# Keys of the latent attention projected with features in rows, tables on ACT and DVE, low parts on Pool

## The chip, the cores and the metric

The kernel runs on one core of one Trainium2 chip. The metric is the device time of one launch in microseconds; the time of the kernel before is the median of 3 runs. The engines are TensorE (PE), VectorE (DVE), ScalarE (ACT), GpSimd (Pool) and the queue that issues transfers (SP).

## What is computed

A decoder of two layers on 256 tokens of width 1024, all in float32. Each layer has three causal attentions side by side and a gated feed-forward part:

```python
h = rms_norm(x, attn_norm)
aq, ak, av, bq, bk, bv, c_q, c_kv_pe, gates = split(h @ w_in)
y_a = diff_attention(aq, ak, av, lam, ...) @ w_branch_a      # 4 heads, two softmaxes each
y_b = dilated_attention(bq, bk, bv, ...) @ w_branch_b        # 4 heads of 128
y_c = mla(c_q, c_kv_pe, ...) @ w_branch_c                    # 8 heads of 64 + 32 rotated
x = x + (g_a * y_a + g_b * y_b + g_c * y_c) @ w_out
x = x + (silu(h2 @ w_ffn_gate) * (h2 @ w_ffn_up)) @ w_ffn_down
```

In `mla` the latent c_q (384) is normalised and expanded to the queries of 8 heads. The latent c_kv (256) is normalised and expanded to 8 heads of 64 key and 64 value features, `kv = (rms_norm(c_kv) @ w_ukv).reshape(B, S, 8, 128)`. A further key part of 32 features is rotated by position and shared by all heads.

## The kernel before

**Products.** Every float32 operand is split in a high part of reduced width and a low part, the rest; a product is three matmuls, high by high, high by low and low by high (`mm3`, `mm` at L210). The high part is made by ACT (`hi_of`, L223) and the low part by DVE, as the source less the high part (`lo_of`, L228, with a scale L230). The weights, 156 MB in all, stream from HBM into five tiles `raw`; ACT makes `whi` from each and DVE `wlo`, five of each.

**Dense stream.** `dense(l)` is a generator. It holds the products of the layer's first half in a fixed order: the latent part of w_in, the projection of queries and keys for a (`qk_proj`, 4 steps), the expansion of the latents (`mla_up`: queries in 3 pieces, keys and values in 2), the values for a (`v_proj`), queries and keys for b, values for b, then the branch products. `pump(n)` runs it for n pieces. Its results stand in four PSUM banks, `bank`; another four, `att`, serve the attention.

**Attention.** `attention()` has 16 units (4 of a, 8 of c, 4 of b), each in stages: scores, softmax terms, transposes of the probabilities, values. The stages run with fixed lags against one another, and after each step one piece of the dense stream is pumped. It begins after 16 pieces of the stream from `latent_scaled` on in layer 0 (1 + 1 + 1 + 13) and 17 in layer 1. A score unit costs DVE two custom instructions (L757), ACT two exponentials (L759).

**Order.** The instructions are not issued in the order of the code: a scheduler of the Tile framework simulates the engines' queues and sets the order on every engine. The order within one queue is then fixed.

**The latent part.** `latent_factors` makes the factors rq and rk of the norms (Pool, L372) and rotates the shared key part on Pool (`rope`, L602 to L605) into `kpe`, from which it is copied to all heads of `k_tm` (L684). `mla_up` projects queries into four banks and scales them by rq into `q_tm`, tokens in rows (L563); Pool rotates their last 32 features in place. Then it projects keys and values together, tokens in rows, in four banks `pu[b][f]`: 24 matmuls of 512 columns in a layer. Each bank is read by ACT for the keys (L588, into `k_tm`, times rk) and by ACT and DVE for the values (into `vc`), and put back at once. `head_pair` (L719) transposes two heads of `q_tm` and two of `k_tm`, 4 transposes each, and splits the results. Pool also makes the distance tables `ta` and `tb` of the scores (L338, L342, L343). `low` are the low parts of the stacked keys for a, DVE's.

## Time and profile before

| | |
|---|---|
| time, median of 3 runs | 883.58 us (883.51 to 883.76) |
| the profiled execution's own time | 883.18 us |
| its span, first to last instruction | 881.4 us |
| PE busy | 873.6 us, 99% |
| DVE busy | 591.1 us, 67% |
| ACT busy | 502.2 us, 57% |
| Pool busy | 71.4 us, 8% |
| mean granted clock of TensorE | 0.999 |

The profile shows one execution. Start times are counted from the span's start. Matmuls overlap in the pipeline, so the time that one takes of PE is the distance between two starts, not its duration. On DVE and ACT too the next instruction starts somewhat before the last one ends.

### The profile page before, as it was taken

The page shows a single profiled execution, that of the slowest core. Times are in us where ns is not written, and L with a number is a line of the kernel's source. Part 1 is how long each engine was busy: PE and PEld are TensorE (multiplying, and loading weights), DVE is VectorE, ACT ScalarE, POOL GpSimd, SP SyncE. Part 2 cuts the span into 40 slices and gives each one's busy share as a digit, 9 for nine tenths or more (in the row PEclk, how much of TensorE's full clock was granted, in tenths as well). Part 3 has the DMA queues.
Part 4 walks back from the last instruction along what each step waited for, and adds up shares of the span by engine and source line. Part 5 has one row for each costly group of instructions (what it writes and reads, how often), then busy time and mean ns, then how long its engine had stood idle before and what let it go on. Part 6 is the DMA issues. An engine that isn't in the chain of part 4 may idle for free.

```text
span 881.4 us, 12736 instructions
## 1 busy us (share of the span) xinstructions
PE 873.6 (99%) x4710; PEld 759.5 (86%) x4710; DVE 591.1 (67%) x990; ACT 502.2 (57%) x852; POOL 71.4 (8%) x95
## 2 busy tenths in 40 slices
PE   9999999999999999999999999999999999999997
PEld 9989988888888888888899899888888888888886
DVE  5988878665666655555467888786556666656444
ACT  7797777644454444444376867775454644444332
POOL 1940310000000000000011303100000000000000
PEclk9999999999999999999999999999999999999999
DMA  9756444456656665656475553444555556655541
GB/s 340 245 170 209 128 141 160 146 169 193 187 167 197 187 190 182 182 186 191 127 226 174 172 168 128 151 145 159 180 189 182 167 193 202 203 190 180 181 141 49
DMA packets 45423, 155.92 MB, mean 177 GB/s; under 512 B 5168, under 2 KB 6192, under 8 KB 45360
## 3 DMA queue, kind: packets, MB, share of 16 engines
q1 hardware_dynamic: 44928, 154.55, 55.0%
q8 instruction: 37, 0.61, 0.3%
q10 hardware_dynamic: 432, 0.55, 0.2%
q14 instruction: 26, 0.21, 0.1%
HBM read 154.03 MB, written 1.05 MB: 176 GB/s over the span
## 4 chain that ended last, share of the span: by engine, by line
PE 97%; POOL 1%; issue 1%; DVE 0%; ACT 0%; POOLq 0%
PE bank L210 87%; PE att L210 6%; PE att L445 2%; PE att L719 1%; PE att L767 0%; PE att L768 0%; PE att L769 0%; POOL f L602 0%; PE att L693 0%; PE att L851 0%; POOL f L604 0%; POOL f L603 0%; POOL q_tm L605 0%; DVE x_tm L1043 0%; ACT x_tm L1058 0%
## 5 line engine op out<-in xcount | busy, mean ns | idle before, releaser
L210 PE MATMUL bank<-whi,fr 128*128 128x512 f32 (+1 forms) x2032 | 631.1, 387 | 0.0
L228 DVE TENSOR_TENSOR wlo<-raw,whi 128x1024 fp32r<-128x1024 f32 (+2 forms) x294 | 353.9, 1206 | 250.8 <-ACT whi L223 250.1
L223 ACT ACTIVATE whi<-raw 128x1024 fp32r<-128x1024 f32 (+2 forms) x294 | 305.0, 1041 | 305.8 <-PE bank L210 246.0
L210 PEld LDWEIGHTS bank<-whi,fr 128*128 128x128 f32 x2032 | 379.8, 188 | 71.5 <-ACT whi L223 0.2
L210 PE MATMUL bank<-wlo,fr 128*128 128x512 f32 (+1 forms) x1016 | 390.1, 386 | 0.0
L210 PEld LDWEIGHTS bank<-wlo,fr 128*128 128x128 f32 x1016 | 191.0, 188 | 35.5 <-DVE wlo L228 0.3
L210 PE MATMUL bank<-fr,whi 128*128 128x256 f32 x512 | 94.6, 285 | 0.0
L210 PEld LDWEIGHTS bank<-fr,whi 128*128 128x128 f32 x512 | 80.0, 192 | 0.2
L210 PE MATMUL bank<-fr,wlo 128*128 128x256 f32 x256 | 73.0, 285 | 0.0
L210 PEld LDWEIGHTS bank<-fr,wlo 128*128 128x128 f32 x256 | 49.0, 192 | 0.0
L372 POOL TENSOR_TENSOR r<-small,mhalf 128x2 f32<-128x2 f32 x4 | 2.8, 708 | 477.5 <-DVE small L398 462.6
L759 ACT ACTIVATE s<-s,small 128x256 f32<-128x256 f32 (+1 forms) x80 | 35.8, 455 | 1.2 <-DVE small L757 0.8
L372 POOL TENSOR_TENSOR small<-small,mhalf 128x2 f32<-128x2 f32 (+1 forms) x12 | 10.0, 831 | 280.5 <-DVE small L1047 178.5
L223 ACT ACTIVATE fr<-att 128x512 fp32r<-128x512 f32 (+2 forms) x54 | 28.3, 559 | 4.1 <-PE att L719 2.3
L210 PE MATMUL att<-whi,fr 128*128 128x288 f32 (+1 forms) x108 | 29.9, 290 | 0.0
L228 DVE TENSOR_TENSOR fr<-att,fr 128x512 fp32r<-128x512 f32 (+2 forms) x46 | 28.2, 634 | 0.1
L223 ACT ACTIVATE fr<-f 64x512 fp32r<-64x512 f32 (+2 forms) x40 | 23.3, 583 | 6.7 <-DVE f L516 5.4
L210 PE MATMUL att<-fr,fr 96*128 96x256 f32 (+3 forms) x152 | 26.0, 277 | 0.0
L210 PEld LDWEIGHTS att<-fr,fr 96*128 96x128 f32 (+1 forms) x152 | 22.7, 190 | 0.6
L615 ACT ACTIVATE f<-bank,rh 128x512 f32<-128x512 f32 x24 | 16.3, 689 | 11.7 <-PE bank L210 11.7
L972 ACT ACTIVATE f<-bank,rh 128x512 f32<-128x512 f32 (+1 forms) x24 | 15.6, 654 | 12.2 <-PE bank L210 12.2
L210 PEld LDWEIGHTS att<-whi,fr 128*128 128x128 f32 x108 | 20.4, 191 | 0.1
(134 smaller groups left out, 636.0 us busy)
## 6 DMA issues: line engine op xcount, KB each, us to landing
raw<-w SPq DMA_DIRECT2D x272, 512.0 KB, 3.6
raw<-w SPq DMA_DIRECT2D x16, 336.0 KB, 3.2
raw<-w SPq DMA_DIRECT2D x6, 384.0 KB, 3.6
x_tm<-xt SPq DMA_DIRECT2D x2, 512.0 KB, 6.4
f<-x SPq DMA_DIRECT2D x3, 256.0 KB, 5.2
f<-fnorm SPq DMA_DIRECT2D x2, 256.0 KB, 4.2
out<-x_tm ACTq DMA_DIRECT2D x2, 256.0 KB, 2.2
f<-x SPq DMA_DIRECT2D x2, 128.0 KB, 3.1
```

Of the source, the lines that this page charges most:

```text
L210: self.nc.tensor.matmul(out, lhsT, rhs, start=start, stop=stop, skip_group_check=True)
L223: self.nc.scalar.activation(out=hi, in_=src, func=AF.Copy, scale=scale)
L228: self.nc.vector.tensor_tensor(out=lo, in0=src, in1=h, op=ALU.subtract)
L372: self.nc.gpsimd.tensor_tensor(out=out, in0=v, in1=self.mhalf[:, 0:v.shape[1]], op=ALU.pow)
L445: self.nc.tensor.transpose(ps[:, c, b * 128:b * 128 + 128], src[b][:, c0 + c * 128:c0 + c * 128 + 128], self.ident)
L615: nc.scalar.activation(out=t[b], in_=bank[b], func=AF.Tanh, scale=self.rh[:, b:b + 1])
L719: nc.tensor.transpose(ps[0:96, c, b * 128:b * 128 + 128], src[:, b, 2 * p + c, :], self.ident)
L759: nc.scalar.activation(out=s[:, SL[b]], in_=s[:, SL[b]], func=AF.Exp, bias=mn[:, b:b + 1], scale=-1.0, accum_out=z[:, b:b + 1])
L972: nc.scalar.activation(out=a, in_=g, func=AF.Tanh, scale=self.rh[:, b:b + 1])
```

## The change

The columns of the kv weights are sorted on the host: keys of all heads first, then values. Keys are projected with features in rows: in each layer 24 matmuls of 256 columns into two banks `pk`, and 12 of 512 for the values into two banks `pv`. The factor rk is applied to the latent beforehand (`latent_factors`, now ahead of the transposes of the latents). Each head's keys are split out of the bank into `kc` (ACT and DVE, 64x256, head by head), the values of a token block in one step of each engine. All four banks are put back after the last split. The rotated key part is transposed (2 transposes a layer) and split into rows 64 to 95 of `kc` (`keys_placed`). `head_pair` transposes queries only. Tables: `ta` on ACT, `tb` on DVE. The low parts of the keys in `low`, and of queries and keys for b, go to Pool (`lo_pool`). The attention begins after 19 pieces in layer 0 (1 + 1 + 1 + 1 + 15) and 20 in layer 1. The last line of the diff gives room in SBUF.

```diff
+    def lo_pool(self, lo, src, hi):
+        self.nc.gpsimd.tensor_tensor(out=lo, in0=src, in1=hi.bitcast(F32), op=ALU.subtract)
...
-        self.k_tm = cp.tile([128, 2, 8, 96], F32, name="k_tm")
+        self.kc = cp.tile([128, 8, 2, 256], F32R, name="kc")
...
-        self.kpe = cp.tile([128, 2, 32], F32, name="kpe")
+        self.kpe = cp.tile([128, 2, 96], F32, name="kpe")
+        nc.gpsimd.memset(self.kpe, 0.0)
...
         for h in range(4):
             t = cp.tile([128, 256], F32, name=f"ta{h}")
-            nc.gpsimd.tensor_scalar(out=t, in0=dm[:, 0:256], scalar1=SLOPE_A[h], scalar2=None, op0=ALU.mult)
+            nc.scalar.activation(out=t, in_=dm[:, 0:256], func=AF.Copy, scale=SLOPE_A[h])
...
         for h in range(4):
             t = cp.tile([128, 256], F32, name=f"tb{h}")
-            nc.gpsimd.tensor_scalar(out=t, in0=db[:, 0:256], scalar1=SLOPE_B[h], scalar2=None, op0=ALU.mult)
-            nc.gpsimd.tensor_tensor(out=t, in0=t, in1=db[:, 256:512], op=ALU.subtract)
+            nc.vector.scalar_tensor_tensor(out=t, in0=db[:, 0:256], scalar=SLOPE_B[h], in1=db[:, 256:512], op0=ALU.mult,
+                                           op1=ALU.subtract)
...
-    def key_pair(self, src, rows=slice(0, 128)):
+    def key_pair(self, src, rows=slice(0, 128), pool=False):
         kd = self.fr.pair()
-        self.split(*fields(kd[rows]), src)
+        hi, lo = fields(kd[rows])
+        self.hi_of(hi, src)
+        (self.lo_pool if pool else self.lo_of)(lo, src, hi)
         return kd
...
         for c in range(2):
             self.hi_of(out[c][halves[1 - c]], t[halves[c]])
-            self.lo_of(self.low[j - 2][c][halves[c]], t[halves[c]], out[c][halves[c]])
+            self.lo_pool(self.low[j - 2][c][halves[c]], t[halves[c]], out[c][halves[c]])
...
             elif j < 2:
                 hi, lo = self.fr.get(), self.fr.get()
-                self.split(hi, lo, t)
+                self.hi_of(hi, t)
+                self.lo_pool(lo, t, hi)
                 q.append((hi, lo))
             else:
-                k.append(self.key_pair(tv))
+                k.append(self.key_pair(tv, pool=True))
             self.f.put(t)
...
         yield
-        pu = [[self.banks.get() for _ in range(2)] for _ in range(2)]
+        banks = [self.banks.get() for _ in range(4)]
+        pk, pv = banks[0:2], banks[2:4]
+        hi, lo = self.ck
         for k in range(2):
             (wh, wl), = self.take()
+            ts = slice(k * 256, k * 256 + 256)
+            for p in range(4):
+                s = slice(p * 128, p * 128 + 128)
+                self.mm3(pk[p // 2][:, (p % 2) * 256:(p % 2) * 256 + 256], wh[:, s], wl[:, s], hi[:, ts], lo[:, ts],
+                         k == 0 and p % 2 == 0, k == 1)
             for b in range(2):
-                h, lo = (t[:, k * 256 + b * 128:k * 256 + b * 128 + 128] for t in self.ck)
-                for lhs, ww, s, e in ((h, wh, k == 0, False), (h, wl, False, False), (lo, wh, False, k == 1)):
-                    for f in range(2):
-                        self.mm(pu[b][f], lhs, ww[:, f * 512:f * 512 + 512], s, e)
+                h, l = (t[:, k * 256 + b * 128:k * 256 + b * 128 + 128] for t in self.ck)
+                self.mm(pv[b], h, wh[:, 512:1024], k == 0, False)
+                self.mm(pv[b], h, wl[:, 512:1024], False, False)
+                self.mm(pv[b], l, wh[:, 512:1024], False, k == 1)
             if k < 1:
                 yield
         self.fr.put(*self.ck)
+        for p in range(4):
+            for c in range(2):
+                src = pk[p // 2][c * 64:c * 64 + 64, (p % 2) * 256:(p % 2) * 256 + 256]
+                self.split(self.kc[0:64, 2 * p + c, 0], self.kc[0:64, 2 * p + c, 1], src)
         for b in range(2):
-            for f in range(2):
-                kv = pu[b][f].rearrange("p (h d) -> p h d", h=4)
-                s = self.rk[:, b:b + 1]
-                nc.scalar.activation(out=self.k_tm[:, b, 4 * f:4 * f + 4, 0:64], in_=kv[:, :, 0:64], func=AF.Copy, scale=s)
-                hi, lo = (self.vc[b][:, 4 * f:4 * f + 4, i] for i in range(2))
-                self.split(hi, lo, kv[:, :, 64:128], s)
-                self.banks.put(pu[b][f])
+            self.split(self.vc[b][:, :, 0], self.vc[b][:, :, 1], pv[b].rearrange("p (h d) -> p h d", h=8))
+        self.banks.put(*banks)
         yield
...
     def latent_factors(self, l):
...
+        for v in (self.vq, self.vk):
+            nc.vector.tensor_scalar(out=v, in0=v, scalar1=EPS, scalar2=None, op0=ALU.add)
         self.rq = self.cp.tile([128, 2], F32, name=f"rq{l}")
-        self.rk = self.cp.tile([128, 2], F32, name=f"rk{l}")
-        rq = self.small()
+        rk, rq = self.small(), self.small()
+        self.rsqrt(rk, self.vk)
         self.rsqrt(rq, self.vq)
-        self.rsqrt(self.rk, self.vk)
+        for b in range(2):
+            nc.vector.tensor_scalar(out=self.cks[b][:, 0:256], in0=self.cks[b][:, 0:256], scalar1=rk[:, b:b + 1],
+                                    scalar2=None, op0=ALU.mult)
         nc.vector.tensor_scalar(out=self.rq, in0=rq, scalar1=-(96 ** -0.5), scalar2=None, op0=ALU.mult)
...
+    def turned_keys(self):
+        nc = self.nc
         for b in range(2):
             t1, t2 = self.f.get(), self.f.get()
-            kp = self.kpe[:, b]
+            kp = self.kpe[:, b, 64:96]
             nc.gpsimd.tensor_copy(kp, self.cks[b][:, 256:288])
             self.rope(kp, t1[:, 0:32], t2[:, 0:32], b, [128])
             self.f.put(t1, t2)
-            nc.gpsimd.tensor_copy(self.k_tm[:, b, :, 64:96], kp.unsqueeze(1).to_broadcast([128, 8, 32]))
+        self.f.put(*self.cks)
+
+    def keys_placed(self):
+        ps = self.att.get()
+        for b in range(2):
+            self.nc.tensor.transpose(ps[0:96, b * 128:b * 128 + 128], self.kpe[:, b], self.ident)
+        src = ps[64:96, 0:256].unsqueeze(1).to_broadcast([32, 4, 256])
+        for h in range(0, 8, 4):
+            self.split(self.kc[64:96, h:h + 4, 0], self.kc[64:96, h:h + 4, 1], src)
+        self.att.put(ps)
...
     def head_pair(self, p):
         nc = self.nc
-        res = []
-        for src in (self.q_tm, self.k_tm):
-            bank = self.att.get()
-            ps = split_rows(bank)
-            for c in range(2):
-                for b in range(2):
-                    nc.tensor.transpose(ps[0:96, c, b * 128:b * 128 + 128], src[:, b, 2 * p + c, :], self.ident)
-            if src is self.k_tm:
-                res.append(self.key_pair(ps[0:96], slice(0, 96)))
-            else:
-                hi, lo = self.fr.get(), self.fr.get()
-                self.split(hi[0:96], lo[0:96], bank[0:96])
-                res.append((hi, lo))
-            self.att.put(bank)
-        return res
+        bank = self.att.get()
+        ps = split_rows(bank)
+        for c in range(2):
+            for b in range(2):
+                nc.tensor.transpose(ps[0:96, c, b * 128:b * 128 + 128], self.q_tm[:, b, 2 * p + c, :], self.ident)
+        hi, lo = self.fr.get(), self.fr.get()
+        self.split(hi[0:96], lo[0:96], bank[0:96])
+        self.att.put(bank)
+        return hi, lo
...
         def scores():
-            q, k = self.pairs[p]
+            q = self.pairs[p]
             cs = slice(c * 256, c * 256 + 256)
-            u["s"] = self.scores((q[0][0:96, cs], q[1][0:96, cs]), k[0:96, c * 512:c * 512 + 512], self.tc_c)
+            u["s"] = self.scores((q[0][0:96, cs], q[1][0:96, cs]), self.kc[0:96, h].rearrange("p f t -> p (f t)"), self.tc_c)
             if c == 1:
                 self.fr.put(*q)
-                self.fr.put(k)
...
             self.latent_scaled()
+            pump(1)
+            self.latent_factors(l)
             if l == 0:
                 self.tables()
                 self.lambdas()
-            pump(1)
+            self.turned_keys()
             self.latent_transposed(l, 0)
             pump(1)
             self.latent_transposed(l, 1)
             pump(1)
             self.latent_transposed(l, 2)
-            self.latent_factors(l)
-            pump(14 if l else 13)
+            pump(1)
+            self.keys_placed()
+            pump(16 if l else 15)
             self.attention(l, pump)
...
+    a["w_ukv"] = a["mla_w_ukv"].reshape(DEPTH, 256, 8, 2, 64).transpose(0, 1, 3, 2, 4).reshape(DEPTH, 256, 1024)
...
-    nc = bacc.Bacc("TRN2", target_bir_lowering=False, num_devices=1)
+    nc = bacc.Bacc("TRN2", target_bir_lowering=False, num_devices=1, dynamic_dma_scratch_size=1024)
```

On PE, layer 0, around the first matmul of `v_proj` for a, before (`bank3` is the bank, `whi1` the weights; `low1_1` belongs to scores of a):

```order
L210 MATMUL att3_68<-low1_1_192,fr7_76 128x128
L719 MATMUL att2_67<-ident_183,q_tm_187 96x128 [waits DVE_49,Pool_49]
L719 MATMUL att2_67<-ident_183,q_tm_187 96x128 [waits Pool_49]
L719 MATMUL att2_67<-ident_183,q_tm_187 96x128 x2
L719 MATMUL att0_65<-ident_183,k_tm_188 96x128 [waits DVE_49,Activation_49]
L210 MATMUL bank3_64<-whi1_143,fr0_69 128x512 [waits DVE_49]
L210 MATMUL bank3_64<-wlo1_148,fr0_69 128x512
L210 MATMUL bank3_64<-whi1_143,fr0_69 128x512 x2
L210 MATMUL bank3_64<-wlo1_148,fr0_69 128x512
```

`v_proj` comes straight after the first transposes of q_tm and k_tm.

The same engine and layer in the changed kernel; `bank1` with `whi0` and `wlo0` is the first piece of the query projection for b:

```order
L210 MATMUL att3_68<-fr10_79,fr7_76 128x128
L210 MATMUL att3_68<-low1_1_192,fr7_76 128x128
L787 MATMUL att2_67<-ident_183,s0_94 128x128 [waits DVE_49]
L788 MATMUL att2_67<-ident_183,s0_94 128x128
L789 MATMUL att2_67<-ident_183,s0_94 128x128
L210 MATMUL bank1_62<-fr0_69,whi0_142 128x256 [waits DVE_49,Activation_49]
L210 MATMUL bank1_62<-fr0_69,whi0_142 128x256
L210 MATMUL bank1_62<-fr0_69,wlo0_147 128x256 [waits DVE_49]
```

A piece of the query projection for b now stands ahead of `v_proj`, and needs `wlo0`. Further down the same queue, `kc` against `fr15` being scores of c:

```order
L210 MATMUL att0_65<-kc_188,fr15_84 128x256 [waits DVE_49]
L210 MATMUL att0_65<-kc_188,fr15_84 128x256 x3
L210 MATMUL att0_65<-kc_188,fr15_84 128x128
L743 MATMUL att2_67<-ident_183,q_tm_187 96x128 [waits DVE_49]
L743 MATMUL att2_67<-ident_183,q_tm_187 96x128 x3
L210 MATMUL bank3_64<-whi1_143,fr0_69 128x512 [waits DVE_49]
L210 MATMUL bank3_64<-wlo1_148,fr0_69 128x512
```

`v_proj` follows the scores of the first c head and the second transposes of q_tm.

On DVE, layer 0, the splits of the values before (`L757` is a score unit of a, `L812` combines two):

```order
L808 RECIPROCAL small15_119<-small14_118 128x2 [waits Activation_49]
L230 SCALAR_TENSOR_TENSOR vc0_185<-bank3_64,rk0_553,vc0_185 128x4x64 [waits Activation_49,Pool_49]
L809 SCALAR_TENSOR_TENSOR small15_119<-small15_119,neglam0_428,small12_116 128x2 [waits DVE_49]
L230 SCALAR_TENSOR_TENSOR vc0_185<-bank0_61,rk0_553,vc0_185 128x4x64 [waits Activation_49]
L812 SCALAR_TENSOR_TENSOR s0_94<-s1_95,small15_119,s0_94 128x256 [waits DVE_49]
L812 SCALAR_TENSOR_TENSOR s0_94<-s1_95,small15_119,s0_94 128x128
L810 RECIPROCAL small22_126<-small18_122 128x2 [waits Activation_49]
L757 ISA s4_98,small23_127<-att1_66,ta2_408 128x256 [waits PE_49]
```

A split of `vc` follows two score units. In the changed kernel (`L777` and `L832` are the same lines, `kc` from `bank3` and `bank0` the keys):

```order
L228 TENSOR_TENSOR wlo4_151<-raw4_141,whi4_146 128x1024 [waits DMAHW6_49,Activation_49]
L777 ISA s1_95,small26_130<-att2_67,ta2_449 128x256 [waits DVE_49,PE_49]
L777 ISA small26_130 128x1
L777 ISA s1_95,small26_130<-att2_67,ta2_449 128x128 [waits DVE_49]
L777 ISA small26_130 128x1
L228 TENSOR_TENSOR vc0_185<-bank1_62,vc0_185 128x8x64 [waits Activation_49]
L228 TENSOR_TENSOR vc1_186<-bank2_63,vc1_186 128x8x64 [waits Activation_49]
L228 TENSOR_TENSOR wlo0_147<-raw0_137,whi0_142 128x1024 [waits DMAHW7_49,Activation_49]
L228 TENSOR_TENSOR kc_188<-bank3_64,kc_188 64x256 [waits Activation_49]
L228 TENSOR_TENSOR kc_188<-bank0_61,kc_188 64x256 [waits Activation_49]
```

The splits of `vc` and `wlo0` stand behind three score units and a weight tile, and the other key splits behind those.

## Rows read from the trace of the kernel before

**Rows 1.** The page's head, granted clock and chain that ended last.
```profile
PE 873.6 (99%) x4710; PEld 759.5 (86%) x4710; DVE 591.1 (67%) x990; ACT 502.2 (57%) x852; POOL 71.4 (8%) x95
...
PEclk9999999999999999999999999999999999999999
...
PE 97%; POOL 1%; issue 1%; DVE 0%; ACT 0%; POOLq 0%
```

**Rows 2.** PE in order of time, layer 0: start us, us, instruction, idle before.
```profile
57.56 0.39 PE L210 MATMUL bank<-wlo,fr 128*128 128x512 f32 x1
57.79 0.62 PE L210 MATMUL bank<-whi,fr 128*128 128x512 f32 x2
...
59.78 0.28 PE L719 MATMUL att<-ident,q_tm 128*96 128x128 f32 x1
60.62 0.54 PE L719 MATMUL att<-ident,q_tm 128*96 128x128 f32 x3 [0.55 <-POOL q_tm L605]
...
61.01 0.47 PE L210 MATMUL bank<-whi,fr 128*128 128x512 f32 x1
```

**Rows 3.** PE in order of time, query projection for a, layer 0.
```profile
26.66 0.40 PE L210 MATMUL bank<-fr,whi 128*128 128x256 f32 x2
26.89 0.28 PE L210 MATMUL bank<-fr,wlo 128*128 128x256 f32 x1
27.02 0.40 PE L210 MATMUL bank<-fr,whi 128*128 128x256 f32 x2
```

**Rows 4.** PE in order of time, q_tm transposes, layer 1.
```profile
494.84 0.61 PE L719 MATMUL att<-ident,q_tm 128*96 128x128 f32 x4
495.28 0.27 PE L719 MATMUL att<-ident,k_tm 128*96 128x128 f32 x1
```

**Rows 5.** DVE in order of time, layer 0.
```profile
57.47 1.55 DVE L228 TENSOR_TENSOR wlo<-raw,whi 128x1024 fp32r<-128x1024 f32 x1
58.94 0.15 DVE L810 RECIPROCAL small<-small 128x2 f32<-128x2 f32 x1
59.02 0.40 DVE L757 CUSTOM_DVE_ANT_0 s<-att,ta 128x256 f32<-128x256 f32 x1
...
59.56 0.41 DVE L757 CUSTOM_DVE_ANT_0 s<-att,ta 128x256 f32<-128x256 f32 x1
...
60.19 0.46 DVE L230 SCALAR_TENSOR_TENSOR vc<-bank,rk,vc 128x256 fp32r<-128x256 f32 x1
60.57 0.21 DVE L809 SCALAR_TENSOR_TENSOR small<-small,neglam,small 128x2 f32<-128x2 f32 x1
...
61.09 0.73 DVE L812 SCALAR_TENSOR_TENSOR s<-s,small,s 128x256 f32<-128x256 f32 x2
```

**Rows 6.** DVE in order of time, layer 1.
```profile
491.83 0.15 DVE L810 RECIPROCAL small<-small 128x2 f32<-128x2 f32 x1
...
496.00 1.22 DVE L228 TENSOR_TENSOR wlo<-raw,whi 128x1024 fp32r<-128x1024 f32 x1
497.14 0.74 DVE L812 SCALAR_TENSOR_TENSOR s<-s,small,s 128x256 f32<-128x256 f32 x2
```

**Rows 7.** DVE's groups by form, 20 to 175 us: count, busy, mean ns.
```profile
L228 DVE TENSOR_TENSOR pt<-att,pt 128x384 fp32r<-128x384 f32 x16 | 8.8, 548 | 0.0
L228 DVE TENSOR_TENSOR fr<-att,fr 96x512 fp32r<-96x512 f32 x8 | 5.3, 676 | 0.0
...
L911 DVE TENSOR_TENSOR f<-att,f 64x256 f32<-64x256 f32 x8 | 3.3, 418 | 2.3 <-ACT f L910 2.2
...
L228 DVE TENSOR_TENSOR low<-f,fr 64x512 fp32r<-64x512 f32 x4 | 2.9, 733 | 0.1
```

**Rows 8.** Pool in order of time, layer 0.
```profile
57.90 1.44 POOL L603 TENSOR_TENSOR f<-q_tm,cs 128x128 f32<-128x128 f32 x1
59.30 0.45 POOL L604 TENSOR_TENSOR f<-q_tm,cs 128x128 f32<-128x128 f32 x1
59.83 0.73 POOL L605 TENSOR_TENSOR q_tm<-f,f 128x256 f32<-128x256 f32 x1
```

More of the change, by code (lines that the diff above doesn't have):

```diff
@@ L65, in weight_plan @@
         block("mla_w_uq", l, 3, 0, 768)
-        block("mla_w_ukv", l, 2, 0, 1024)
+        block("w_ukv", l, 2, 0, 1024)
         block("w_in", l, KT, OFF_AV, 512)
@@ L669, in latent_factors @@
         nc = self.nc
-        nc.vector.tensor_scalar(out=self.vq, in0=self.vq, scalar1=EPS, scalar2=None, op0=ALU.add)
-        nc.vector.tensor_scalar(out=self.vk, in0=self.vk, scalar1=EPS, scalar2=None, op0=ALU.add)
+        for v in (self.vq, self.vk):
+            nc.vector.tensor_scalar(out=v, in0=v, scalar1=EPS, scalar2=None, op0=ALU.add)
         self.rq = self.cp.tile([128, 2], F32, name=f"rq{l}")
-        self.rk = self.cp.tile([128, 2], F32, name=f"rk{l}")
-        rq = self.small()
+        rk, rq = self.small(), self.small()
+        self.rsqrt(rk, self.vk)
         self.rsqrt(rq, self.vq)
-        self.rsqrt(self.rk, self.vk)
+        for b in range(2):
+            nc.vector.tensor_scalar(out=self.cks[b][:, 0:256], in0=self.cks[b][:, 0:256], scalar1=rk[:, b:b + 1],
+                                    scalar2=None, op0=ALU.mult)
         nc.vector.tensor_scalar(out=self.rq, in0=rq, scalar1=-(96 ** -0.5), scalar2=None, op0=ALU.mult)
+    def turned_keys(self):
+        nc = self.nc
         for b in range(2):
             t1, t2 = self.f.get(), self.f.get()
-            kp = self.kpe[:, b]
+            kp = self.kpe[:, b, 64:96]
             nc.gpsimd.tensor_copy(kp, self.cks[b][:, 256:288])
@@ L708, in latent_transposed @@
             self.ck = (hi, lo)
-            self.f.put(*self.cks)
     def head_pair(self, p):
         nc = self.nc
-        res = []
-        for src in (self.q_tm, self.k_tm):
-            bank = self.att.get()
-            ps = split_rows(bank)
-            for c in range(2):
-                for b in range(2):
-                    nc.tensor.transpose(ps[0:96, c, b * 128:b * 128 + 128], src[:, b, 2 * p + c, :], self.ident)
-            if src is self.k_tm:
-                res.append(self.key_pair(ps[0:96], slice(0, 96)))
-            else:
-                hi, lo = self.fr.get(), self.fr.get()
-                self.split(hi[0:96], lo[0:96], bank[0:96])
-                res.append((hi, lo))
-            self.att.put(bank)
-        return res
+        bank = self.att.get()
[7 more added lines that the diff above has]
+        return hi, lo
     def scores(self, q, k, table):
```

## The prediction

> **What bounds the kernel now.** I read the page's head first, then the chain that ended last, then PE's order of time, then the engines that feed PE. TensorE (PE) is busy 99% of the span, the chain of waits is PE for 97%, and the granted clock stands at its full level, 2.4 GHz, throughout [rows 1]. So the time is PE's work plus the places where PE stands still. I went through PE's order of time for these. There is one of any size: the first transposes of the latent queries in layer 0. The first issues at 59.78 us, the other three at 60.62 [rows 2]; one takes 0.11 [rows 4], so about **0.7 us** is lost, to Pool's rotation of q_tm, which starts its last step at 59.83 and needs 0.73 for it [rows 8]. In layer 1 the same place runs through without a gap [rows 4]. A change can thus win in two ways only, by taking work from PE and by closing that gap, and it loses wherever PE comes to wait for ACT, DVE or Pool.
>
> How near those waits are is seen at v_proj for a. In layer 0 its first matmul issues at 61.01 [rows 2], into the bank that DVE's split of vc, begun at 60.19, has just read [rows 5]. So around 60 us the feeding engines have no reserve, though they have some elsewhere.
>
> **Work on PE.** Removed: 32 transposes of k_tm (4 pairs of 4, two layers). Added: 4 of kpe. At 0.11 each (494.84 to 495.28 for four [rows 4]) that is 28 x 0.11 = 3.1 us less. The kv product gives up 24 matmuls of 512 columns and takes 48 of 256 over the program. A 512-column matmul issues every 0.23 us (57.56 to 57.79 [rows 2]), a 256-column one every 0.12 (three from 26.66 to 27.02 [rows 3]): 48 x 0.12 - 24 x 0.23 = +0.2. Sum **-2.8 us**, all on the path, since PE is the path.
>
> **Work that only matters if PE waits for it.** Per layer DVE gets 8 splits of keys (64x256), 2 of the rotated part (32x4x256), 2 wider vc splits and 2 scalings of cks, and in layer 0 four tables; it loses 4 low parts (0.73 each [rows 7]), 4 splits of k_tm, 4 small vc splits and 4 low parts of b. The two lists nearly cancel in layer 0, and DVE gains some 2 us in layer 1. ACT gets about as much as it loses. The tables (about 0.4 each on either engine) cost PE nothing so long as they are there at the first score unit; the eight steps stand far ahead of it on both queues, beside PE's work on the latents. The cks scalings now come before the transposes of the latents; those have other dense pieces ahead of them, so I put them at nothing, up to 0.7 if Pool's factor is late. The low parts for b are wanted tens of us after they are made: nothing.
>
> **What PE comes to wait for in layer 0.** The edit of mla_up splits the keys head by head, high part on ACT, then low part on DVE, and puts all four banks back only after the last split. v_proj, which before took two banks as soon as they were read, takes the key banks. The order on PE shows the answer of the scheduler: ahead of v_proj stands a piece of the query projection for b, 24 matmuls of 256 columns, which itself needs vc0 (its bank) and a low weight tile, wlo0, from DVE. Both are late on DVE's queue. I follow that queue from 58.94, where the wlo begun at 57.47 lets the next step start [rows 5]; the ACT order ahead of the matching wlo is the same q_tm and weight steps as before, so I keep that time. From there to the end of wlo0, with durations from start to start: three reciprocals and a small product 0.4; the combined pair of s0 0.7 (0.73 [rows 5]); two key splits 0.7 (0.42 each, 0.08 of it overlapped as in 60.19 to 60.57 [rows 5, 7]); two score units of 0.54 (59.02 to 59.56 [rows 5]) 1.1; wlo4 1.14 (496.00 to 497.14 [rows 6]); one more unit 0.54; vc0 and vc1 at 0.6 (nearest: the 96x512 split, 0.68 less overlap [rows 7]) 1.2; wlo0 1.14. Together 6.9, so wlo0 ends at **65.9**.
>
> When would PE ask for it? Its first q_tm transposes began at 59.78 [rows 2]. In the new order 0.3 us more lies ahead of them (12 matmuls of 512 columns became 24 of 256, +0.1; two kpe transposes, +0.2), and behind them come four transposes (0.4), eight score matmuls (4 x 0.12 + 4 x 0.06 = 0.7) and three transposes (0.3): **61.6**. So PE waits 65.9 - 61.6 = **4.3 us**, some of it already at the score matmuls, whose att banks wait for the same units. The old 0.7 lies inside this and goes. After wlo0 PE has 24 x 0.12 + 0.5 + 0.4 = 3.8 us of work, to 69.7. DVE meanwhile does four key splits, a 96x512 split, a 128x384 one (0.55 [rows 7]), a pair and small steps, and then the last split of bank3: 0.7 + 0.6 + 0.5 + 0.7 + 0.7 + 0.5 + 0.3 = 4.0, also to 69.9. v_proj follows with hardly a further wait.
>
> Bounds: with DVE a whole us earlier 3.3, a whole us later 5.3.
>
> **And in layer 1.** The same with another order: the piece of b waits for wlo2, behind four score units, vc0, vc1 and kc splits. From 491.83, where the step behind the matching wlo starts [rows 6]: small steps 0.3, three key splits 1.0, a pair 0.7, wlo1 1.14, four units 2.2, two vc 1.2, wlo2 1.14: 7.7, to 499.5. PE's transposes began at 494.84 [rows 4]; with the same 0.9 of work behind them it asks at 495.7. Wait: **3.8 us**. Layer 1 has no old gap to close. Bounds 2.8 to 4.8.
>
> **Pool.** The low parts of keys for a (four a layer, 64x512) now stand on Pool ahead of the rotation of q_tm. No such step is in the trace; by twice the 128x256 one (0.73 [rows 8]) it is some 1.5. Beside a wlo, Pool is held: a 128x128 product took 1.44 (57.90) where the next took 0.45 (59.30) [rows 8], and the wlo of 57.47 took 1.55 where that of 496.00 took 1.22 [rows 5, 6]. So the rotation may end 1 to 2 us later than 60.6; that is still before 65.9 and inside the wait already counted. It costs only if the wlo's on DVE's queue are each held up by 0.33 as well, three in a layer: up to +1.0 per layer. The Trainium skill's page "SBUF — State Buffer", section "Who interferes with whom", says that a DVE instruction with two SBUF inputs and a Pool instruction that reads SBUF exclude one another, the one that starts first holding the shared port for its whole length. The two long rows agree that they disturb each other. By that rule a wlo could be held for a whole Pool step of 1.5, and with one such meeting a layer the sum would be 887.8 + 3.0 = 890.8; a weaker form of it, with the 0.33 of the rows, is the third rival.
>
> **Sum.** The profiled run took 883.18 us, 1.8 above its span, and 0.4 below the median of 883.58; I forecast on the profiled run: 883.18 - 2.8 - 0.7 + 4.3 + 3.8 = **887.8 us**.
>
> **Rivals.**
> 1. *The feeding engines are in time.* If DVE, relieved of the low parts before this place, reaches the end of its wlo's 4 us sooner than I assume, nothing is waited for and the saved work shows: 883.18 - 2.8 - 0.7 = 879.7. For it: it runs beside PE for 20 us before this, with the three later steps of attention to spare. Against: the wlo's are tied to weight tiles that PE itself frees. It decides from a DVE lead of about 4 us. This is the faster side.
> 2. *Only layer 0 waits.* In layer 1 DVE is freer by 2 us, and if wlo2 is reached by 495.7 that term goes: 887.8 - 3.8 = 884.0, no change that can be told.
> 3. *Pool and DVE hold each other up* in both layers, 1.0 each: 889.8. For it the two long rows of 57.47 and 57.90; against, that DVE has fewer of these steps itself.
> 4. *The change does not do what it says*: the scheduler leaves the transposes or the 512-column products in. The order on PE excludes that.
>
> **Chances.** Forecast 0.55 (886 to 889), rival 1 0.20, rival 2 0.15, rival 3 0.10. A difference of 0.2%, 1.8 us, is about what a measurement of this kernel can tell from none. Faster: 0.20. Same: 0.15. Slower: 0.55 + 0.10 = 0.65. The range must reach rival 1, since cutting it off would leave out 2 in 10 with nothing for the ends: 879.5 to 890.0.
>
> **What will show it.** In the new profile PE should stand still at the first matmuls of the b piece ahead of v_proj, some 4 us in layer 0 and in layer 1, released by DVE's wlo or vc split, and PE's busy time should be some 2.8 us less. The gap at q_tm released by Pool should be gone or swallowed. If PE goes through there without a gap, my time for DVE's queue is wrong and rival 1 holds. If the wait ends on Pool, rival 3 does. If DVE's 64x256 splits take far from 0.42, or the 32x4x256 ones far more than twice that, the sums of both layers move with them.

## The result: 9.7 us slower, twice what was forecast

The changed kernel takes 893.46 us (median of 5 runs, 891.91 to 895.11) against 883.76 us before in the same comparison; the ratio is 1.0112, with a 95% interval of 1.0098 to 1.0126. The forecast was 887.8 us, with a range to 890.0: the right way, at about half the size. The profiled execution took 893.08 us, 9.9 more than that of before.

The page of the profile after, head, granted clock in 40 slices, chain that ended last:

```profile
PE 876.9 (98%) x4706; PEld 759.8 (85%) x4706; DVE 593.0 (67%) x990; ACT 504.9 (57%) x856; POOL 79.1 (9%) x96
...
PEclk9998999999999999999999999999999999999999
...
PE 93%; DVE 3%; DMA 2%; issue 1%; ACT 1%; SPq 0%; POOLq 0%; POOL 0%; DVEq 0%; ACTq 0%
PE bank L210 84%; PE att L210 5%; PE att L449 2%; DVE wlo L228 1%; DMA raw<-w 1%; DMA f<-x 1%; DVE s L777 1%; PE att L787 0%; PE att L788 0%; PE att L789 0%; PE att L743 0%; DVE vc L228 0%; PE att L720 0%; ACT whi L223 0%; DVE kc L228 0%
```

PE does less now on the chain (93%; [rows 1] had 97%), and DVE has come in with 3%: `wlo`, score units, `vc`. The clock row has an 8 in its fourth slice, where [rows 1] has only 9s. That is 67 to 89 us.

PE in order of time, layer 0 (start us, us, instruction, idle before and what ended it), which answers to [rows 2]:

```profile
62.12 0.61 PE L743 MATMUL att<-ident,q_tm 128*96 128x128 f32 x4
63.37 0.39 PE L210 MATMUL att<-fr,fr 128*128 128x256 f32 x1 [0.64 <-DVE small L777]
...
65.62 0.33 PE L787 MATMUL att<-ident,s 128*128 128x128 f32 x1 [1.01 <-DVE small L777]
...
66.31 0.77 PE L210 MATMUL bank<-fr,whi 128*128 128x256 f32 x2
67.95 0.58 PE L210 MATMUL bank<-fr,wlo 128*128 128x256 f32 x1 [0.87 <-DVE wlo L228]
68.33 0.63 PE L210 MATMUL bank<-fr,whi 128*128 128x256 f32 x2
...
68.97 0.63 PE L210 MATMUL bank<-fr,whi 128*128 128x256 f32 x2
...
73.66 0.48 PE L210 MATMUL bank<-whi,fr 128*128 128x512 f32 x1
```

and layer 1, which answers to [rows 4]:

```profile
501.50 0.28 PE L210 MATMUL att<-low,fr 128*128 128x128 f32 x1
503.29 0.61 PE L743 MATMUL att<-ident,q_tm 128*96 128x128 f32 x4 [1.52 <-DVE small L777]
504.33 0.39 PE L210 MATMUL att<-fr,fr 128*128 128x256 f32 x1 [0.43 <-DVE small L777]
...
506.64 0.33 PE L787 MATMUL att<-ident,s 128*128 128x128 f32 x1 [0.48 <-DVE small L777]
...
507.78 0.39 PE L210 MATMUL bank<-fr,wlo 128*128 128x256 f32 x1 [0.59 <-DVE wlo L228]
508.01 0.40 PE L210 MATMUL bank<-fr,whi 128*128 128x256 f32 x2
...
508.36 0.40 PE L210 MATMUL bank<-fr,whi 128*128 128x256 f32 x2
...
511.40 0.49 PE L210 MATMUL bank<-whi,fr 128*128 128x512 f32 x1
```

Both of the forecast waits are there, at the place forecast: the score matmuls, the transposes of s0 and the b piece ahead of `v_proj`, each released by DVE. In layer 0 the first transposes of q_tm start at 62.12; with 1.47 us of work behind them and two matmuls of 0.12 the first low matmul of the b piece is due at 63.8, and it starts at 67.95: **4.1 us** (forecast 4.3). In layer 1 the last score set ends at 501.6, 1.7 us of work follow, and the low matmul comes at 507.78 in place of 503.3: **4.5 us** (forecast 3.8). The gap that Pool's rotation left in [rows 2] is gone, as forecast.

What was not forecast stands behind the wait of layer 0. Three 256-column matmuls take 0.64 us (68.33 to 68.97), against 0.36 in [rows 3]; in layer 1, at the same place, 0.35 (508.01 to 508.36). `v_proj` follows 5.7 us behind the low matmul in layer 0, 3.6 in layer 1. The stretches of the profile after show why (time, PE and its weight loads, DVE, ACT, Pool busy, granted clock, DMA share, GB/s):

```profile
60.00:65.00 5.00, 3.96 (x28) 3.34 (x26) 4.96 (x19) 4.95 (x13) 1.88 (x3) 1.00 0.64 209
65.00:66.00 1.00, 0.38 (x3) 0.31 (x3) 1.00 (x6) 1.00 (x4) 0.00 (x0) 0.94 0.01 4
66.00:67.00 1.00, 1.00 (x4) 0.50 (x2) 1.00 (x3) 1.00 (x5) 0.00 (x0) 0.50 0.65 193
...
71.00:72.00 1.00, 1.00 (x7) 1.00 (x7) 0.97 (x3) 0.00 (x0) 0.00 (x0) 0.50 0.07 29
72.00:73.00 1.00, 1.00 (x7) 1.00 (x7) 0.76 (x3) 0.11 (x1) 0.00 (x0) 0.64 0.00 0
...
505.00:510.00 5.00, 3.91 (x28) 3.36 (x28) 4.94 (x19) 3.61 (x15) 0.00 (x0) 1.00 0.24 66
```

The granted clock stood at half, 1.2 of 2.4 GHz, from 66 us, in the middle of the wait, until past 72. PE had been busy 3.96 us of the 5 before 65, and 0.38 of the one from 65 to 66. That costs 5.7 - 3.6 = **2.1 us**. Such a drop to half is called a fall of the clock below.

The sum from these rows: -2.8 of work, -0.7 of the old gap, +4.1 and +4.5 of waits, +2.1 of the clock, and +2.0 lost in the first 25 us (the first transposes of q_tm at 62.12 against 59.78 before, less the forecast 0.3): 9.2 of the 9.9. The missing 0.7 is in the work. The transposes of x_tm between the layers and the last matmul, first before, then after:

```profile
444.18 1.03 PE L445 MATMUL att<-ident,x_tm 128*128 128x128 f32 x8
...
874.93 0.28 PE L210 MATMUL att<-whi,fr 128*128 128x256 f32 x1
```

```profile
450.52 1.03 PE L449 MATMUL att<-ident,x_tm 128*128 128x128 f32 x8
...
884.83 0.28 PE L210 MATMUL att<-whi,fr 128*128 128x256 f32 x1
```

Layer 1 takes 434.31 us in place of 430.75. That is 3.6 more with a wait of 4.5, so its work is 0.9 less and not half of 2.8. Layer 0 takes 6.3 more; its other terms are 2.0 + 4.1 + 2.1 - 0.7 = 7.5, so its work is 1.2 less. What is left over for the work is thus -2.1.

Of the 2.0 of the first 25 us, 1.4 lies at two waits for weights:

```profile
22.20 0.50 PE L210 MATMUL bank<-fr,whi 128*128 128x256 f32 x2 [0.36 <-ACT whi L223]
...
23.46 0.39 PE L210 MATMUL bank<-fr,wlo 128*128 128x256 f32 x1 [0.46 <-DVE wlo L228]
```

They belong to this execution: the profile of the first run below has the same matmuls in the same order up to 94 us and neither wait, and its transposes of kpe start at 38.37 where these start at 39.88. The other four executions had mean clocks of 0.991 to 0.995 (the profiled one 0.995; before: 0.998 and 0.999) and so lost as much or more to the clock. How many falls each had was not recorded; the first run below has two in its profile, at a mean clock of 0.992.

### The profile page after: what moved, and what is told of

It is laid out like the page before. It is cut to its first block, busy times and chain, and to the rows that moved or that the text cites. A ratio compares the mean times of both kernels' runs of the same rounds, so it can differ in the third digit from the quotient of the medians.

```text
span 891.3 us, 12747 instructions
## 1 busy us (share of the span) xinstructions
PE 876.9 (98%) x4706; PEld 759.8 (85%) x4706; DVE 593.0 (67%) x990; ACT 504.9 (57%) x856; POOL 79.1 (9%) x96
## 4 chain that ended last, share of the span: by engine, by line
PE 93%; DVE 3%; DMA 2%; issue 1%; ACT 1%; SPq 0%; POOLq 0%; POOL 0%; DVEq 0%; ACTq 0%
PE bank L210 84%; PE att L210 5%; PE att L449 2%; DVE wlo L228 1%; DMA raw<-w 1%; DMA f<-x 1%; DVE s L777 1%; PE att L787 0%; PE att L788 0%; PE att L789 0%; PE att L743 0%; DVE vc L228 0%; PE att L720 0%; ACT whi L223 0%; DVE kc L228 0%
## 5 line engine op out<-in xcount | busy, mean ns | idle before, releaser
L210 PE MATMUL bank<-whi,fr 128*128 128x512 f32 (+2 forms) x2016 | 629.2, 387 | 0.8 <-ACT whi L223 0.8
L210 PE MATMUL bank<-wlo,fr 128*128 128x512 f32 (+2 forms) x1008 | 387.9, 386 | 0.0
L210 PE MATMUL bank<-fr,whi 128*128 128x256 f32 x544 | 102.2, 289 | 0.4 <-ACT whi L223 0.4
L210 PEld LDWEIGHTS bank<-fr,whi 128*128 128x128 f32 x544 | 86.7, 196 | 1.2 <-ACT whi L223 0.6
L210 PE MATMUL bank<-fr,wlo 128*128 128x256 f32 x272 | 78.6, 289 | 1.9 <-DVE wlo L228 1.9
L210 PEld LDWEIGHTS bank<-fr,wlo 128*128 128x128 f32 x272 | 53.2, 196 | 2.7 <-DVE wlo L228 2.6
L223 ACT ACTIVATE fr<-att 128x512 fp32r<-128x512 f32 (+2 forms) x46 | 24.0, 553 | 3.0 <-PE att L743 1.4
L228 DVE TENSOR_TENSOR fr<-att,fr 128x512 fp32r<-128x512 f32 (+2 forms) x38 | 23.0, 626 | 0.3 <-ACT fr L223 0.3
L233 POOL TENSOR_TENSOR fr<-f,fr 128x512 fp32r<-128x512 f32 x8 | 14.2, 1772 | 81.4 <-ACT fr L223 81.4
L223 ACT ACTIVATE pt<-att 128x384 fp32r<-128x384 f32 x32 | 15.4, 485 | 9.7 <-PE att L789 9.5
```

The source lines that it names most:

```text
L210: self.nc.tensor.matmul(out, lhsT, rhs, start=start, stop=stop, skip_group_check=True)
L223: self.nc.scalar.activation(out=hi, in_=src, func=AF.Copy, scale=scale)
L228: self.nc.vector.tensor_tensor(out=lo, in0=src, in1=h, op=ALU.subtract)
L233: self.nc.gpsimd.tensor_tensor(out=lo, in0=src, in1=hi.bitcast(F32), op=ALU.subtract)
```

## The experiments

My theory after this reading: PE waits some 4 us a layer for DVE, because the key and value splits stand on its full queue among score units and weights; behind such a wait the clock falls. The rivals were the later start of the attention, Pool's low parts, and too little DVE time in whatever order.

**The attention begun three steps earlier again.**

```diff
-            pump(16 if l else 15)
+            pump(13 if l else 12)
```

> The changed kernel with the attention begun after 16 and 17 pieces again, three fewer than the change has. Theory (DVE's queue at the keys and values: PE waits some 4 us in each layer for splits and low weights that stand behind them, whatever the step at which the attention is begun, because the scheduler puts the first units of a at the same place of PE's order): 893, within 1.5 of the changed kernel. Rival (the later start has pushed the score units onto the key and value splits): the wait shrinks to under 1.5 us in each layer, 884 to 887.

Measured: 893.33 us, ratio 1.0109 (1.0094 to 1.0124): the theory. PE's order around the place is the same row by row. The scheduler sets it by what is ready in its own reckoning, and the step at which the code calls the attention hardly matters. Its profile, in the stretches used above, shows the clock at half in layer 1 too:

```profile
65.00:70.00 5.00, 4.13 (x19) 3.67 (x18) 4.94 (x15) 2.41 (x9) 0.00 (x0) 0.50 0.59 206
...
505.00:510.00 5.00, 4.77 (x21) 4.37 (x22) 4.91 (x16) 2.45 (x8) 0.00 (x0) 0.50 0.33 104
```

**Low parts on DVE again.**

```diff
     def lo_pool(self, lo, src, hi):
-        self.nc.gpsimd.tensor_tensor(...)
+        self.nc.vector.tensor_tensor(...)
```

> The changed kernel with the low parts of the keys for a, and of queries and keys for b, on DVE again instead of Pool. Theory (order of DVE's queue at the keys and values): the low parts stand ahead of the place where DVE has spare time, so the waits stay near 4 us a layer, 892 to 895. Rival (Pool and DVE hold each other up): without Pool's steps the low weights come 1 us a layer earlier, 890 to 891. Second rival (DVE has too little time altogether): 2.9 us more of DVE work a layer make the waits longer by as much, 897 to 899.

Measured: 892.36 us, 1.0094 (1.0077 to 1.0111), 1.0 less than the run above on the same chip, with intervals that overlap. The theory's range; 16 more steps on DVE in the two layers did no harm.

**Values first, banks put back one by one.**

```diff
+        for b in range(2):
+            self.split(self.vc[b][:, :, 0], self.vc[b][:, :, 1], ...)
+            self.banks.put(pv[b])
         for p in range(4):
...
-        self.banks.put(*banks)
+            if p % 2:
+                self.banks.put(pk[p // 2])
```

> The changed kernel with the values split first and each bank put back after its own last reader: values, then keys of heads 0 to 3, then 4 to 7. The value projection for a then takes the two value banks, and the piece of b moves behind it. Theory (PE waits for the key splits and for what stands among them): the waits fall to under 1 us in each layer, the clock stays at full level, 881 to 885. Rival (DVE has too little time there, in whatever order): the waits only move, 889 to 893.

Measured: 889.22 us, 1.0056 (1.0038 to 1.0074), on the rival's edge. `v_proj` moved ahead of the b piece and the wait for `wlo0` went, but the waits of the score sets and transposes for DVE's score units stayed, 2.2 and 2.3 us, and the clock fell behind both in the profiled execution (0.66 in 65 to 70 us, 0.70 in 500 to 505). Its four executions give a price of the clock: 886.24 us at a mean clock of 0.998, 889.10 at 0.996, 889.34 and 889.65 at 0.994.

**The keys alone**, tables on Pool, low parts on DVE, start as before:

```diff
-            nc.scalar.activation(out=t, in_=dm[:, 0:256], func=AF.Copy, scale=SLOPE_A[h])
+            nc.gpsimd.tensor_scalar(out=t, in0=dm[:, 0:256], scalar1=SLOPE_A[h], ...)
...
-            pump(16 if l else 15)
+            pump(13 if l else 12)
```

> The new key projection alone: tables on Pool, low parts on DVE and the start of the attention as before. Theory (the key and value splits with four banks put back at the end do it): both waits are there, 890 to 896. Rival (tables and low parts, moved onto DVE's and Pool's queues, do it): 881 to 884.

Measured: 896.85 us, 1.0145 (1.013 to 1.016): the theory, and 3.4 more than with all parts. Part of that is a wait of its own, at 44 us: the rotated key part comes late behind Pool's tables, as this row of PE shows; I had put that at nothing to 0.7 for the whole change, where the tables are off Pool:

```profile
43.82 0.31 PE L707 MATMUL att<-ident,kpe 128*96 128x128 f32 x1 [1.73 <-POOL kpe L618]
```

**Keys split when their pair is due.**

```diff
-        for p in range(4):
-            for c in range(2):
-                ...
+        self.key_banks = pk
...
         def pre():
             if c == 0:
+                self.keys_split(p)
                 self.pairs[p] = self.head_pair(p)
```

> The changed kernel with each pair of heads' keys split out of the bank only when the attention comes to that pair (two heads on ACT and DVE, just ahead of its transposes), the value banks put back as they are read, the key banks after their second pair. The same work, spread out. Theory (DVE and ACT are full where 16 key splits, 4 value splits, the weights' parts and the first score units of a meet, and PE waits for DVE there): the waits fall from some 4 to 1 or 2 us a layer, and where they are short the clock stays at its full level: 880 to 885. Rival (the score units of a alone fill DVE there, the key splits only come on top): 886 to 890, as with the values first.

Measured: 891.98 us, 1.0085 (1.0071 to 1.01): worse than the rival. The waits around the score sets stay (0.77 and 1.23 us in layer 0, 2.3 in layer 1), the clock falls once (0.66 in 65 to 70 us), and a wait of 1.5 us at 81 us is new, where later keys are now split.

**The same, and query low parts of a on Pool.**

```diff
-                self.lo_of(out[c][halves[1 - c]], t[halves[c]], out[c][halves[c]])
+                self.lo_pool(out[c][halves[1 - c]], t[halves[c]], out[c][halves[c]])
```

> As the run with the keys split late, and in addition the low parts of the stacked queries for a (four 64x512 a layer, 0.93 us each on DVE) on Pool. Theory (DVE has too little time from the projection for a up to the values for a): 1 to 3 us less than that run, 878 to 883. Rival (Pool then holds DVE up, or brings the rotation of the queries late): the same or 1 to 3 us more.

Measured: 892.21 us, 1.0092 (1.0078 to 1.0107): the rival's number, but not its place. The wait has moved ahead of the query transposes, and it is a DVE score unit that ends it, not Pool:

```profile
65.56 1.06 PE L748 MATMUL att<-ident,q_tm 128*96 128x128 f32 x4 [3.87 <-DVE small L782]
```

**The other parts without the keys**: the kernel before with tables on ACT and DVE and the low parts on Pool.

```diff
-                self.split(hi, lo, t)
+                self.hi_of(hi, t)
+                self.lo_pool(lo, t, hi)
...
-                k.append(self.key_pair(tv))
+                k.append(self.key_pair(tv, pool=True))
```

> The kernel before with only the other parts of the change: tables on ACT and DVE, low parts of the keys for a and of queries and keys for b on Pool; keys as before. Theory (the new key projection makes the waits): within 1 us of the kernel before, 882.5 to 884.5. Rival (Pool's low parts bring the rotation of the queries late, where PE already waited 0.7): 884.5 to 887.

Measured: 883.46 us, 0.9996 (0.9986 to 1.0005): no change. The theory. The old gap of 0.7 is closed here too, and 0.5 is lost ahead of it: the transposes of q_tm start at 60.27 in place of 59.78. The other parts without the keys lose nothing, and the keys without the other parts lose 13: so the loss comes with the keys.

**Waits alone.** The kernel before, with low parts of four weight tiles in the feed-forward part written many times over:

```diff
             self.split(self.whi[j][:, :n], self.wlo[j][:, :n], self.raw[i % N_RAW][:, :n])
+            for _ in range(HELD.get(i, 0)):
+                self.lo_of(self.wlo[j][:, :n], self.raw[i % N_RAW][:, :n], self.whi[j][:, :n])
```

> The kernel before, with four weight tiles of the feed-forward part whose low part DVE writes 10, 11, 12 and 13 times over in place of once, so that PE has to wait there, nothing else changed. With 1.15 us a step and some 8.7 us by which these tiles are made ahead, PE should wait some 2, 3, 4 and 5 us. Theory (the granted clock falls to half behind a wait of some 3 us or more, and PE's work costs 2 to 3 us more before it rises again): the time grows by the waits and by 2 to 3 us for each of the longer ones, to 902 to 908. Rival (a wait costs its own length, and the clock fell in the changed kernel for another reason, such as 256-column matmuls): the granted clock stays at 1.00 and the time grows by the waits alone, to 896 to 898.

Measured: 911.98 us, 1.0316 (1.0302 to 1.033). The time is more than I expected since the waits are longer and come in several pieces, but the question is answered by the clock. Stretches around the second wait (1.8 us longer than a matmul's own interval, at 360), the third (4.5 us, to 701.6) and the fourth (7.5 us, to 786.1):

```profile
358.00:360.00 2.00, 0.68 (x4) 0.22 (x2) 2.00 (x2) 1.96 (x3) 0.00 (x0) 1.00 0.28 113
360.00:362.00 2.00, 1.68 (x7) 1.42 (x8) 2.00 (x4) 0.35 (x1) 0.00 (x0) 1.00 0.86 268
362.00:364.00 2.00, 2.00 (x10) 1.63 (x10) 1.91 (x3) 0.00 (x0) 0.00 (x0) 1.00 0.85 262
698.00:702.00 4.00, 0.36 (x1) 0.36 (x2) 3.58 (x4) 0.36 (x1) 0.00 (x0) 0.66 0.55 156
702.00:704.00 2.00, 2.00 (x6) 1.52 (x6) 0.00 (x0) 0.00 (x0) 0.00 (x0) 0.50 0.87 293
...
706.00:708.00 2.00, 2.00 (x10) 1.58 (x9) 0.63 (x1) 1.06 (x1) 0.00 (x0) 0.98 0.00 0
784.00:786.00 2.00, 0.00 (x0) 0.00 (x0) 1.97 (x2) 0.00 (x0) 0.00 (x0) 0.50 0.00 0
788.00:790.00 2.00, 2.00 (x6) 1.61 (x5) 0.00 (x0) 0.00 (x0) 0.00 (x0) 0.50 0.34 133
792.00:796.00 4.00, 4.00 (x20) 3.29 (x19) 3.53 (x4) 1.13 (x2) 0.00 (x0) 1.00 0.41 131
```

Behind the short wait the clock stays at full level. In the two long ones it falls to half before PE goes on, and it is up again in the rows from 706 and from 792. There PE's 512-column matmuls stand 0.43 apart:

```profile
701.64 0.79 PE L211 MATMUL bank<-wlo,fr 128*128 128x512 f32 x1 [4.37 <-DVE wlo L229]
702.23 0.63 PE L211 MATMUL bank<-whi,fr 128*128 128x512 f32 x1
...
705.64 0.83 PE L211 MATMUL bank<-whi,fr 128*128 128x512 f32 x2
```

From 702.23 to 705.64 there are eight, 3.41 us, in place of 8 x 0.23 = 1.8. The first wait, 1.9 us and a second one of 0.9 behind it, also ended in a fall (0.91 in 288 to 290, 0.50 in 290 to 292). Nothing of the changed kernel is in this one: a wait is enough. From the end of the wait to the first matmul at full pace, against 0.23 for each matmul and the 0.1 by which the first is longer behind the short wait too, the three falls cost 1.6 us (289.22 to 293.19, ten matmuls), 2.1 (701.64 to 706.31, eleven) and 2.5 (786.11 to 791.88, fourteen), on top of the wait.

**The rotated part split once and spread by a transfer**, with the keys split late:

```diff
-        for h in range(0, 8, 4):
-            self.split(self.kc[64:96, h:h + 4, 0], self.kc[64:96, h:h + 4, 1], src)
+        self.split(kr[:, 0], kr[:, 1], ps[64:96, 0:256])
+        self.nc.scalar.dma_start(out=self.kc[64:96].bitcast(F32),
+            in_=kr.bitcast(F32).unsqueeze(1).to_broadcast([32, 8, 2, 256]))
```

> The run with the keys split late, and the rotated key part split once (32x256) and spread to the eight heads by a transfer, in place of two 32x4x256 splits on ACT and DVE. DVE loses some 2 us of work a layer and ACT 1.7 ahead of the score units, PE's order has the values for a ahead of more of the units. Theory (DVE and ACT are full from the projection for a to the values for a): the waits shrink to under 2 us a layer, 882 to 887. Rival (the transfer comes late behind the weights' transfers, or the wait moves to Pool's rotation of the queries): 888 to 892.

Measured: 886.69 us, 1.0029 (1.0017 to 1.004): the theory, 5.3 less than with the keys split late alone. The waits are 2.0 us in layer 0 and 1.6 in layer 1, and in the profiled execution the clock stays at 1.00 behind both. The clock again tells the executions apart: 885.12 and 885.20 us at 0.999, 886.62 to 887.15 at 0.997, 888.61 at 0.994.

**The same, low parts of the keys for a on DVE.**

```diff
-            self.lo_pool(self.low[j - 2][c][halves[c]], t[halves[c]], out[c][halves[c]])
+            self.lo_of(self.low[j - 2][c][halves[c]], t[halves[c]], out[c][halves[c]])
```

> As the run with the transfer, and the low parts of the keys for a (four 64x512 a layer) on DVE again; those for b stay on Pool. Theory (Pool's 64x512 steps hold DVE's steps with two SBUF sources, and bring the rotation of the queries late, by as much as they save): 1 to 2 us less than that run, 880 to 885. Rival (they relieve DVE): 1 to 3 us more than that run.

Measured: 887.41 us, 1.0037 (1.0023 to 1.0051): no difference from the run above that counts, so neither. In its profile the clock falls behind a wait of 1.9 us in layer 0 (0.50 in 64 to 67 us). The rows of the two runs show why these steps are worth so little on Pool. DVE in order of time, two query low parts, first with the keys' low parts on Pool at the same time, then without, and between them Pool's steps:

```profile
43.33 3.52 DVE L228 TENSOR_TENSOR fr<-f,fr 64x512 fp32r<-64x512 f32 x2
```

```profile
43.31 3.00 POOL L233 TENSOR_TENSOR low<-f,fr 64x512 fp32r<-64x512 f32 x2 [6.68 <-ACT fr L223]
```

```profile
43.62 1.41 DVE L228 TENSOR_TENSOR fr<-f,fr 64x512 fp32r<-64x512 f32 x2
```

The same two DVE steps take 3.52 and 1.41 us: 2.1 lost to Pool's first pair. Four such steps are 2.9 us of DVE's work, so most of what Pool takes over is lost again. The Trainium skill's page "SBUF — State Buffer", section "Who interferes with whom", has the port that the two engines share as an exclusive lock, which a DVE instruction with two SBUF inputs and a Pool instruction that reads SBUF contend for. The trace agrees: beside Pool's two steps of 1.5 us each DVE step takes 1.1 longer than alone.

**Without the low parts of the keys.**

```diff
-                self.split(self.kc[0:64, 2 * p + c, 0], self.kc[0:64, 2 * p + c, 1], src)
+                self.hi_of(self.kc[0:64, 2 * p + c, 0], src)
```

> The changed kernel without the low parts of the keys out of the key banks: the eight 64x256 steps a layer on DVE are left out, the low parts are zero. Everything else, and all matmuls, stay. Theory (these steps, behind one another with ACT's and in front of the low weights on DVE's queue, are what PE waits for): the value projection for a comes straight behind the query transposes again, the waits shrink from 4 to under 1.5 us a layer, and the clock stays at its full level: 881 to 885. Rival (the rest of DVE's and ACT's work at this place, the score units and weights, is too much already): 888 to 892.

Measured: 882.09 us, 0.998 (0.9971 to 0.9989), 0.2% faster than before, with the keys' low parts left at zero. PE runs through the place without a gap, `v_proj` straight behind the query transposes, and the clock stays up:

```profile
62.45 0.61 PE L744 MATMUL att<-ident,q_tm 128*96 128x128 f32 x4
62.81 0.48 PE L210 MATMUL bank<-whi,fr 128*128 128x512 f32 x1
```

```profile
60.00:65.00 5.00, 5.00 (x31) 4.35 (x30) 4.84 (x20) 4.88 (x13) 2.20 (x3) 1.00 0.74 222
65.00:70.00 5.00, 5.00 (x24) 4.15 (x23) 4.75 (x12) 5.00 (x16) 0.00 (x0) 1.00 0.59 143
...
505.00:510.00 5.00, 5.00 (x37) 4.69 (x36) 4.39 (x7) 3.15 (x7) 0.00 (x0) 1.00 0.90 279
```

Eight DVE steps of 0.42 us a layer (3.1 us of work in layer 0) were the difference between no wait and 4 us. Part of their effect is the order: without them `v_proj` stands ahead of the piece of b that needs `wlo0`. How much is the order and how much DVE's time this run does not separate. The 1.8 us below before also stand against a forecast of 3.5 for work and old gap; layer 1, which has no wait here, takes 430.19 us (444.69 to 874.88) in place of 430.75.

**The split called at the first scores**, in the run with the transfer:

```diff
         def pre():
             if c == 0:
-                self.keys_split(p)
                 self.pairs[p] = self.head_pair(p)
...
             q = self.pairs[p]
+            if c == 0:
+                self.keys_split(p)
```

> The run with the transfer, with each pair's key split called for only at the pair's first scores instead of two steps earlier. Theory (what stands on DVE's queue among the score units of a makes PE wait, and the scheduler would put the later call later): the wait at the query transposes falls from 2.0 to some 1 us in layer 0, 884 to 886. Rival (the scheduler puts a step wherever an engine is free in its own reckoning, so the place of the call in the code decides little): 886 to 888.

Measured: 886.20 us, 1.0025 (1.0013 to 1.0036): as in the run with the transfer, the rival. As with the step at which the attention begins, the place of the call decides little. The waits are again 2.0 us in layer 0 and 1.6 in layer 1, and now the clock falls behind the shorter one. PE's rows there, and a stretch behind them:

```profile
497.14 0.61 PE L749 MATMUL att<-ident,q_tm 128*96 128x128 f32 x4 [0.84 <-DVE small L783]
498.18 0.39 PE L210 MATMUL att<-fr,fr 128*128 128x256 f32 x1 [0.43 <-DVE small L783]
```

```profile
499.00:502.00 3.00, 3.00 (x8) 2.32 (x8) 3.00 (x13) 2.98 (x14) 0.00 (x0) 0.50 0.03 7
```

So the length of a wait does not tell whether the clock falls: 1.6 us in two pieces did it here, and 2.0 in two pieces did not, in layer 0 of this same execution. The theory of 3 us and more, which the run with the waits alone was to test, had its limit too high.

No version with the keys in rows and all of the work beat the kernel before. The nearest, 886.69 and 886.20, still wait 3.6 us in all at the score units.

## Why the forecast was right in kind and wrong in size

- *Less work on PE, -2.8.* The direction was right, the size too large: -2.1 is left for it in the profile after, and layer 1 of the run that leaves the low parts out is 0.6 shorter where 1.4 was due. The number of matmuls is as counted (4706 against 4710); what takes the rest back is not shown.
- *The wait in layer 0, 4.3.* Measured 4.1. The row lengths held: the 64x256 split takes 0.415 on DVE (nearest row 0.418 in [rows 7]), the value split 0.672. That the wait came so near is in part luck. From the end of the wlo's to the end of wlo0 it was 7.6 us in place of 6.9, since the pair that [rows 5] has at 0.73 took 1.34; but DVE began this stretch 0.7 earlier, counted from PE's transposes, than I had it (60.27 against 62.12; forecast 58.94 against 60.1).
- *The wait in layer 1, 3.8.* Measured 4.5, and again errors offset each other. I let PE have 0.9 us of work from the start of the transposes, where layer 0 had 1.4 and the rows after have 1.7; with 1.7 the sum gives 3.0. DVE's stretch was 8.6 us (499.13 to 507.7) in place of 7.7, and it began 0.5 later, counted as for layer 0.
- *The old gap.* Gone.
- *Behind the wait.* This step failed. I wrote that after wlo0 PE has 3.8 us of work, to 69.7, and so priced it at full clock, as in every row that I had, and let the wait cost its own length. It took 5.7 in layer 0, at half the granted clock for most of it; in the run with the attention begun earlier, whose order on PE is the same there, the clock stood at half in layer 1 too. My bounds had no term for it: the kernel before never waits long enough to show it, since the only gap of [rows 2] is 0.7. With the sizes measured, the sum is 887.8 + 0.7 (work) - 0.2 + 0.7 (waits) + 2.1 (clock) + 2.0 (first 25 us) = 893.1, the profiled execution (the work is what was left over, so it must close). Both waits lie within their bounds; without the fall and without the 1.4 us of waits for weights that execution would have come out at 889.6, inside the range.
- *Pool.* The estimate of 1.5 for a 64x512 step held (1.42 in the mean), and the rotation was not what PE waited for. The 0.33 that I took for a meeting with DVE was too small: a wlo begun at 52.00 beside Pool's low part took 2.32 us, where one alone takes 1.2. That is near the 1.5 by which I let a whole Pool step hold a wlo, but the run with the low parts back on DVE is only 1.0 faster, with intervals that overlap.
- *Rivals.* That all is in time (879.7) fell, as did that of layer 0 alone (884.0). That of Pool and DVE (889.8) has the direction but is not the cause: with the low parts back on DVE both waits stay.

What stays open is how many of the 9.7 us of the median are falls of the clock, since only the profiled execution's stretches were recorded, and what decides whether a wait brings the clock down.

## What to carry to other kernels

Where one engine is busy 99% and its feeders are full, moving a conversion earlier and into one place can cost more than the main engine saves: follow the feeding queue by name through that place, as the sum here did. Then give each wait of TensorE of the size seen here (1.6 us in all and more) a range: the granted clock may fall with it, and a fall cost 1.6 to 2.5 us on top of the wait's own length, or nothing where it did not come. A call's place in the code is no handle on the order where a scheduler sets it; what an engine has to do is.

## What the runs showed of the hardware

- The granted clock fell to 1.2 GHz with waits of PE of 4.5 and 7.5 us and stayed there for the first microseconds of the work behind. It did not with one of 1.8, but did with two of 1.9 and 0.9 with little between them. With waits of 4.1 and 4.5 in one execution it fell in layer 0 and not in layer 1; with 2.0 and 1.6 in another it fell with the shorter alone. A fall cost 1.6 to 2.5 us.
- Two DVE steps with two SBUF sources (64x512) took 3.52 us beside Pool's steps of the same kind and 1.41 without.
- A Pool subtraction of 64x512 took 1.42 us in the mean of eight, of 128x512 1.77; the shortest of each, in the run without the keys, are both 1.28, so half the partitions did not halve the time.
